# Hybrid block on one core: the attention's heads chained into one pipeline of key blocks, and the reciprocals of a query block spread over later steps

## The chip, the cores and the metric

One core of a Trainium2 chip runs the whole program. The metric is device time in microseconds; a run's time is that of one execution, and three runs of the kernel before are at hand. The engines are named as in the profile: PE (TensorE) does matmuls and PEld loads their stationary operand, DVE is VectorE, ACT is ScalarE, POOL is GpSimd, SP is SyncE, which here only issues DMAs. Each engine works off its own queue in order.

## The reference, cut to what matters

One decoder block on 1024 tokens of width 1024: a gated mix of an attention with forgetting and a state-space branch (S5), an output projection, then a mixture of 32 experts. The change touches only the attention, which has 8 heads of 64:

```python
qf = q * d ** -0.5                       # q, k normalised per head before
logits = einsum('bhqd,bhkd->bhqk', qb, kf) + cb[..., :, None] - cum[:, :, None, :]
logits = where(pos[None, :] <= pb[:, None], logits, -1e30)     # causal
p = softmax(logits, axis=-1)
o = einsum('bhqk,bhkd->bhqd', p, vf)
mixed = sigmoid(g_attn) * (y_attn @ w_proj_attn) + sigmoid(g_ssm) * (y_ssm @ w_proj_ssm)
```

## The kernel before, in words

Every fp32 product is made of parts: an operand is split into a high part, rounded to the fp32r type by ACT, and a low part, the rest, by DVE. Tiles whose names end in h (or H) and l (or L) are such pairs.

The attention works on four pairs of heads. For a pair, `proj` makes q, k and v of 128 tokens at a time (24 matmuls, L798 to L800, in a PSUM tile of `psA`); ACT and DVE take v out into the tile `V` (L809, L810). `prep` does one half of the tokens (512): it transposes k and q into two PSUM tiles of `psB` (L824, L827), ACT and DVE write them out as `KX`, `KY`, `QX`, `QY` (L836 to L842), and then it finds each query's largest logit, by matmuls into `psB` tiles (L855, with the causal mask L858) that DVE reduces (L860, tile `mx`); the maxima are transposed (L865), and POOL sends them by DMA into rows of `QX` (L871, L872).

`attend(pair, c)` takes the 512 queries of half c against 4c + 4 blocks of 128 keys, first for head a = 0 of the pair, then for a = 1. A unit of it is one key block: the logits in a `psB` tile (L904, L907, with the mask L906), two exponentials by ACT, `pH` (L910) and `pe` (L912; for the first block it goes to `sm`), the low part `pL` by DVE (L913), and the running sum of the exponentials, `sm`, by POOL (L915). The products with the values (L889 with `pH`, L890 with `pL`, summed in the `psA` tile `acc`) come three key blocks later, from a list `late`. At the end of a head the last three are emitted at once; then `yu` is written from `acc` (ACT L923, DVE L924), and `sm` is split into `sh` (ACT L926) and `sl` (DVE L928). After both heads, four matmuls (L933) with a selecting matrix sum `sh` and `sl` over the partitions into a tile of `psA`; DVE takes its reciprocals in four parts, each followed by a multiplication into `yu` (L936, L937); POOL stores `yu` to HBM (L944). `pL` and `sl` share four buffers, `yu` has one, `sm` two. `psA` and `psB` have four PSUM banks each.

`run_all` interleaves generators: each has a number of units and a stretch of the run [lo, hi], and the one whose next unit is due first goes on. One call runs `attend(cur, 0)` beside `proj` of the next pair and `prep(cur, 1)`, the next `attend(cur, 1)` beside `proj` and `prep` of the next pair. In the last pair the partner is `fill`: the products of the other branch's output (L703 to L705 with `wm` and `yhs`, DVE L728 writes `mixS`). After the last call come the products with `yha` (L703 to L705 again), of which the last key group needs the last pair's result (`y3`, DVE L942), and `emit_a` (DVE L991).

The code is not the order of the engines. A scheduler under it takes the instructions in program order as priority, models their times, gives out tile buffers and lets a later instruction pass one whose inputs or buffer are not there. So the place of an instruction in its engine's queue has to be read from the compiled program.

Of the kernel before, what the change touches and what calls it, by code (L numbers as in the profile page):

```python
# [10 lines left out]
F32 = mybir.dt.float32  # L11
# [31 lines left out]
def hybrid_block(ctx: ExitStack, tc: tile.TileContext, t, out):  # L43
# [728 lines left out]
    def new_pair(pr):  # L772
        p_ = Pair()
        p_.pr = pr
        p_.w = proj_weights(pr)
        p_.V = ap_.tile([P, NT, 2, 2, 64], F32R, name="V", bufs=2)
        p_.KX, p_.KY, p_.QX, p_.QY = [], [], {}, {}
        for a in range(2):
            kx = slot("KX", dt=F32R)
            ky = slot("KY", dt=F32R)  # L780
            nc.sync.dma_start(f32(kx[64:68, :]), negF_d[2 * pr + a])
            p_.KX.append(kx)
            p_.KY.append(ky)
        return p_

    def proj(p_, half):
# [4 lines left out]
        for r in range(4):  # L791
# [15 lines left out]
            vs = ps[:, 256:384].rearrange("p (a b) -> p a b", b=64)  # L807
            vh = p_.V[:, i, :, 0, :]
# [64 lines left out]

    def attend(p_, c, last=None):
# [3 lines left out]
        yu = ap_.tile([P, 512], F32, name="yu", bufs=1)  # L878
        sums = []
        for a in range(2):  # L880
            kx, qx, ky, qy = p_.KX[a], p_.QX[a, c], p_.KY[a], p_.QY[a, c]

            acc = psA.tile([P, 512], F32, tag="A", name="acc")
            sm = ap_.tile([P, 512], F32, name="sm", bufs=2)

            def values(kt, o0, n, pH, pL):
                v = p_.V[:, kt, a].rearrange("p a b -> p (a b)")
                o = acc[:, o0:o0 + n]
                nc.tensor.matmul(o, v, pH[:, :n], start=(kt == 0), stop=False)  # L889
                nc.tensor.matmul(o, v, pL[:, :n], start=False, stop=(kt == nkt - 1))  # L890

            late = []
            for kt in range(nkt):
# [17 lines left out]
                pe = ap_.tile([P, 512], F32, name="pe", bufs=3) if kt else sm  # L911
                nc.scalar.activation(pe[:, :n], ps[:, :n], AF.Exp)  # L912
                nc.vector.tensor_tensor(pL[:, :n], pe[:, :n], f32(pH[:, :n]), ALU.subtract)  # L913
                if kt:
                    nc.gpsimd.tensor_tensor(sm[:, o0:], sm[:, o0:], pe[:, :n], ALU.add)  # L915
# [6 lines left out]
            orow = slice(a * 64, a * 64 + 64)  # L922
            nc.scalar.copy(yu[orow, :], acc[0:64, :])  # L923
            nc.vector.tensor_tensor(yu[orow, :], yu[orow, :], acc[64:128, :], ALU.add)  # L924
            sh = ap_.tile([P, 512], F32R, name="sh", bufs=1)
            nc.scalar.copy(sh, sm)  # L926
            sl = ap_.tile([P, 512], F32R, tag="pL", name="sl", bufs=4)
            nc.vector.tensor_tensor(sl, sm, f32(sh), ALU.subtract)  # L928
            sums += [(a, sh), (a, sl)]
            yield  # L930
        ps = smtile() if last is not None else mmtile()
        for j, (a, v) in enumerate(sums):
            nc.tensor.matmul(ps, sel[:, a], v, start=(j == 0), stop=(j == 3))  # L933
        for q in range(4):
            qs = slice(q * P, q * P + P)
            nc.vector.reciprocal(ps[:, qs], ps[:, qs])  # L936
            nc.vector.tensor_tensor(yu[:, qs], ps[:, qs], yu[:, qs], ALU.mult)  # L937
        if last is not None:
            last.append((slot("yha", dt=F32R), slot("yla", dt=F32R)))
            yh, yl = last[-1]  # L940
            nc.scalar.copy(yh[:, 512:S], yu)
            nc.vector.tensor_tensor(yl[:, 512:S], yu, f32(yh[:, 512:S]), ALU.subtract)  # L942
            return
        nc.gpsimd.dma_start(yaT_d[p_.pr * P:(p_.pr + 1) * P, c * 512:c * 512 + 512], yu)  # L944
# [4 lines left out]
    for pr in range(4):  # L949
        if pr < 3:  # L950
            nxt = new_pair(pr + 1)
            run_all((attend(cur, 0), 10, 0.1, 1), (proj(nxt, 0), 12, 0, 1), (prep(cur, 1), 10, 0.25, 1))
            if pr < 2:
                run_all((attend(cur, 1), 18, 0.1, 1), (proj(nxt, 1), 12, 0, 1), (prep(nxt, 0), 10, 0.3, 1))
            else:
                fill = mixed_ssm()
                run_all((attend(cur, 1), 18, 0.1, 1), (proj(nxt, 1), 12, 0, 0.9), (prep(nxt, 0), 10, 0.3, 1),
                        (itertools.islice(fill, 5), 5, 0.9, 1.1))
# [593 lines left out]
```

## Time and profile before

| | |
|---|---|
| median of 3 runs | 1171.51 us (1167.63 to 1173.89) |
| the profiled execution | 1170.5 us, its span 1168.8 us, granted TensorE clock 0.981 |
| PE, PEld busy | 1106.3 us (95%), 848.5 us (73%) |
| DVE, ACT, POOL busy | 805.0 us (69%), 620.4 us (53%), 353.4 us (30%) |
| first and last logits of the attention (L904) | 356.2 and 635.7 us |
| experts | from about 840 us to the end |

The span runs from the first to the last instruction. A busy share is a mean over stages with different limits, so the stretch of the attention has to be asked for by itself. Matmuls overlap, so a matmul's duration is longer than the distance to the next one's start; idle time of PE stands in square brackets behind the row that ended it, with the releaser.

### The profile page before, as it was taken

The page shows a single profiled execution, that of the slowest core. Times are in us where ns is not written, and L with a number is a line of the kernel's source. Part 1 is how long each engine was busy: PE and PEld are TensorE (multiplying, and loading weights), DVE is VectorE, ACT ScalarE, POOL GpSimd, SP SyncE. Part 2 cuts the span into 40 slices and gives each one's busy share as a digit, 9 for nine tenths or more (in the row PEclk, how much of TensorE's full clock was granted, in tenths as well). Part 3 has the DMA queues.
Part 4 walks back from the last instruction along what each step waited for, and adds up shares of the span by engine and source line. Part 5 has one row for each costly group of instructions (what it writes and reads, how often), then busy time and mean ns, then how long its engine had stood idle before and what let it go on. Part 6 is the DMA issues. An engine that isn't in the chain of part 4 may idle for free. (4 is left out here: it accounts for less than half of the span.)

```text
span 1168.8 us, 15930 instructions
## 1 busy us (share of the span) xinstructions
PE 1106.3 (95%) x5323; PEld 848.5 (73%) x5324; DVE 805.0 (69%) x1594; ACT 620.4 (53%) x1195; POOL 353.4 (30%) x400
## 2 busy tenths in 40 slices
PE   6999999999999999999999989997799999999995
PEld 5787878887897888788667868786566666666562
DVE  6949878964147899898996795538666666666560
ACT  6433233333246666658878442113567777676562
POOL 4101011013144665747434351202222222222211
PEclk9999999999999999999999998999799999999998
DMA  8544553321704030002524548545899999999992
GB/s 250 78 110 120 129 82 83 82 73 54 153 17 55 12 65 11 16 10 82 208 82 136 183 152 299 182 164 200 281 330 339 321 314 308 316 312 320 320 335 50
DMA packets 100918, 193.78 MB, mean 166 GB/s; under 512 B 26176, under 2 KB 55168, under 8 KB 100832
## 3 DMA queue, kind: packets, MB, share of 16 engines
q1 hardware_dynamic: 82176, 150.16, 42.1%
q0 software_dynamic: 14048, 34.17, 10.8%
q10 hardware_dynamic: 4608, 8.39, 1.9%
q8 instruction: 43, 0.70, 0.2%
q14 instruction: 43, 0.35, 0.1%
HBM read 164.30 MB, written 35.52 MB: 171 GB/s over the span
## 5 line engine op out<-in xcount | busy, mean ns | idle before, releaser
L1126 DVE TENSOR_TENSOR wel<-raw_e,weh 128x512 fp32r<-128x512 f32 x248 | 152.3, 685 | 118.3 <-ACT weh L1125 114.5
L1125 ACT CAST weh<-raw_e 128x512 fp32r<-128x512 f32 x248 | 132.7, 623 | 1.6 <-DMA raw_e<-in_w_expert_up 1.5
L1404 PE MATMUL psA_t<-wd,hT 128*96 128x512 f32 x256 | 117.2, 600 | 2.8 <-DMA wd<-in_w_expert_down 2.0
L915 POOL TENSOR_TENSOR sm<-sm,pe 128x256 f32<-128x256 f32 (+2 forms) x80 | 96.2, 1202 | 68.6 <-ACT pe L912 60.4
L1379 PE MATMUL psA_t<-weh,xh 128*96 128x512 f32 x256 | 103.2, 403 | 0.2
L1380 PE MATMUL psA_t<-wel,xh 128*96 128x512 f32 x256 | 101.0, 395 | 0.0
L1381 PE MATMUL psA_t<-weh,xl 128*96 128x512 f32 x256 | 101.0, 394 | 0.0
L162 PE MATMUL psA_t<-hTl,wgh 128*128 128x512 f32 x256 | 100.6, 393 | 0.0
L161 PE MATMUL psA_t<-hTh,wgl 128*128 128x512 f32 x256 | 100.5, 393 | 0.0
L160 PE MATMUL psA_t<-hTh,wgh 128*128 128x512 f32 x256 | 100.4, 392 | 0.0
L798 PE MATMUL psA_t<-wqh,hTh 128*128 128x384 f32 x256 | 87.9, 343 | 0.0
L799 PE MATMUL psA_t<-wql,hTh 128*128 128x384 f32 x256 | 86.3, 337 | 0.0
L800 PE MATMUL psA_t<-wqh,hTl 128*128 128x384 f32 x256 | 86.2, 337 | 0.0
L1406 POOL DMA_INDIRECT out_rows<-R,ix x32 | 46.1, 1441 | 128.3 <-ACT hT L1395 117.1
L1405 ACT ACTIVATE R<-psA_t,wts 96x512 f32<-96x512 f32 x64 | 43.7, 682 | 77.0 <-PE psA_t L1404 74.9
L1404 PEld LDWEIGHTS psA_t<-wd,hT 128*96 128x96 f32 x256 | 40.4, 168 | 55.5 <-issue 50.4
L1355 POOL DMA_INDIRECT XG<-xn_d,ix x32 | 32.1, 1002 | 136.3 <-PE psB_t L1366 129.6
L910 ACT ACTIVATE pH<-psB_t 128x512 fp32r<-128x512 f32 (+1 forms) x96 | 49.3, 513 | 35.8 <-PE psB_t L907 35.6
L913 DVE TENSOR_TENSOR pL<-pe,pH 128x256 fp32r<-128x256 f32 (+2 forms) x80 | 62.6, 794 | 6.1 <-ACT pe L912 5.2
L164 ACT COPY ge<-psA_t 128x512 f32<-128x512 f32 x32 | 18.6, 582 | 70.1 <-PE psA_t L162 70.1
L161 PEld LDWEIGHTS psA_t<-hTh,wgl 128*128 128x128 f32 x256 | 48.1, 188 | 9.7
L160 PEld LDWEIGHTS psA_t<-hTh,wgh 128*128 128x128 f32 x256 | 48.1, 188 | 9.6
(429 smaller groups left out, 2845.5 us busy)
## 6 DMA issues: line engine op xcount, KB each, us to landing
raw_e<-in_w_expert_gate SPq DMA_DIRECT2D x64, 512.0 KB
raw_e<-in_w_expert_up SPq DMA_DIRECT2D x64, 512.0 KB
wd<-in_w_expert_down SPq DMA_DIRECT2D x64, 512.0 KB
gate_d<-ge ACTq DMA_DIRECT2D x32, 256.0 KB
gt<-gate_d SPq DMA_DIRECT2D x16, 512.0 KB
raw_g<-in_w_in SPq DMA_DIRECT2D x12, 512.0 KB
raw_q<-in_w_in SPq DMA_DIRECT2D x48, 128.0 KB
x<-in_x SPq DMA_DIRECT2D x8, 512.0 KB
```

What stands on the lines that cost most here:

```text
L160: nc.tensor.matmul(ps, wh, hTh[k][:, ns], start=(k == 0), stop=False)
L161: nc.tensor.matmul(ps, wl, hTh[k][:, ns], start=False, stop=False)
L162: nc.tensor.matmul(ps, wh, hTl[k][:, ns], start=False, stop=(k == KD - 1))
L798: nc.tensor.matmul(ps[:, :384], ah, wh, start=(k == 0), stop=False)
L799: nc.tensor.matmul(ps[:, :384], ah, wl, start=False, stop=False)
L915: nc.gpsimd.tensor_tensor(sm[:, o0:], sm[:, o0:], pe[:, :n], ALU.add)
L1125: nc.scalar.copy(wh[d_], src)
L1126: nc.vector.tensor_tensor(wl[d_], src, f32(wh[d_]), ALU.subtract)
L1379: nc.tensor.matmul(ps, xh[:, k, :], wh[:, k % 2, :], start=(k == 0), stop=False)
L1380: nc.tensor.matmul(ps, xh[:, k, :], wl[:, k % 2, :], start=False, stop=False)
L1381: last = nc.tensor.matmul(ps, xl[:, k, :], wh[:, k % 2, :], start=False, stop=(k == KD - 1))
L1404: pe = nc.tensor.matmul(po, hT[:, j, :], wd[j][:, ns], start=(j == 0), stop=(j == 1))
```

## The change

The list `late` is no longer a head's own: it goes across heads, calls of `attend` and pairs. So a head's last three products with the values are emitted in the first units of whatever head comes next. What followed them at the end of a head (`done`: `yu`, `sh`, `sl`) comes when the last of them has been emitted, and the sums over the partitions (`add_up`) are made for each head by itself: `sh` and `sl` of head 0 start a tile, those of head 1 finish it. That tile now comes from `psB` in all calls, not from `psA`. The four reciprocals with their multiplications are dealt out to the next four units (`later`), and the store of `yu` follows the last of them, which lies in the next call of `attend`. `yu` is taken from its one buffer when the first head is done; `V` when the first tokens of a pair are written. The last call drains the lists in units of its own. The numbers given to `run_all` change too: attention counts 8 and 16 units (24 in the last call), and the starts of the stretches move.

```diff
-        p_.V = ap_.tile([P, NT, 2, 2, 64], F32R, name="V", bufs=2)
+        p_.V = None
...
+            if p_.V is None:
+                assert all(v[0] >= p_.pr - 1 for v in late)
+                p_.V = ap_.tile([P, NT, 2, 2, 64], F32R, name="V", bufs=2)
...
+    late, later = [], []
+    def advance(depth):
+        while len(late) > depth:
+            late.pop(0)[1]()
+            if depth:
+                break
+        for v in list(later):
+            v[0] -= 1
+            if v[0] <= 0:
+                later.remove(v)
+                v[1]()
...
     def attend(p_, c, last=None):
-        yu = ap_.tile([P, 512], F32, name="yu", bufs=1)
-        sums = []
+        b = Block()
+        b.yu = None
+        def values(h, a, kt, o0, n, pH, pL):
+            if kt == 0:
+                h.acc = psA.tile([P, 512], F32, tag="A", name="acc")
...
+            if kt == nkt - 1:
+                done(h, a)
+        def done(h, a):
+            if b.yu is None:
+                b.yu = ap_.tile([P, 512], F32, name="yu", bufs=1)
+            orow = slice(a * 64, a * 64 + 64)
+            nc.scalar.copy(b.yu[orow, :], h.acc[0:64, :])
+            nc.vector.tensor_tensor(b.yu[orow, :], b.yu[orow, :], h.acc[64:128, :], ALU.add)
+            sh = ap_.tile([P, 512], F32R, name="sh", bufs=1)
+            nc.scalar.copy(sh, h.sm)
+            sl = ap_.tile([P, 512], F32R, tag="pL", name="sl", bufs=4)
+            nc.vector.tensor_tensor(sl, h.sm, f32(sh), ALU.subtract)
+            later.append([1, lambda: add_up(b, a, (sh, sl))])
+        def add_up(b, a, vs):
+            if a == 0:
+                b.ps = smtile()
+            for j, v in enumerate(vs):
+                nc.tensor.matmul(b.ps, sel[:, a], v, start=(a + j == 0), stop=(a + j == 2))
+            if a:
+                for q in range(4):
+                    later.append([1 + q, lambda q=q: scaled(b, q)])
+        def scaled(b, q):
+            qs = slice(q * P, q * P + P)
+            nc.vector.reciprocal(b.ps[:, qs], b.ps[:, qs])
+            nc.vector.tensor_tensor(b.yu[:, qs], b.ps[:, qs], b.yu[:, qs], ALU.mult)
+            if q == 3:
+                result(b)
...
-                late.append((kt, o0, n, pH, pL))
-                if len(late) > 3:
-                    values(*late.pop(0))
+                late.append((p_.pr, lambda h=h, a=a, v=(kt, o0, n, pH, pL): values(h, a, *v)))
+                advance(3)
                 yield
-            for v in late:
-                values(*v)
...
-        ps = smtile() if last is not None else mmtile()
-        for j, (a, v) in enumerate(sums):
-            nc.tensor.matmul(ps, sel[:, a], v, start=(j == 0), stop=(j == 3))
...
+        if last is not None:
+            while late or later:
+                advance(len(late) - 1 if len(late) > 1 else 0)
+                yield
...
-            run_all((attend(cur, 0), 10, 0.1, 1), (proj(nxt, 0), 12, 0, 1), (prep(cur, 1), 10, 0.25, 1))
+            run_all((attend(cur, 0), 8, 0, 1), (proj(nxt, 0), 12, 0.15, 1), (prep(cur, 1), 10, 0.25, 1))
-                run_all((attend(cur, 1), 18, 0.1, 1), (proj(nxt, 1), 12, 0, 1), (prep(nxt, 0), 10, 0.3, 1))
+                run_all((attend(cur, 1), 16, 0.05, 1), (proj(nxt, 1), 12, 0, 1), (prep(nxt, 0), 10, 0.3, 1))
...
-            run_all((attend(cur, 0), 10, 0, 1), (itertools.islice(fill, 16), 16, 0, 1),
+            run_all((attend(cur, 0), 8, 0, 1), (itertools.islice(fill, 16), 16, 0, 1),
-            run_all((attend(cur, 1, y3), 18, 0.1, 1), (fill, 32, 0, 1), (ready_a(), 5, 0.5, 0.95))
+            run_all((attend(cur, 1, y3), 16 + 8, 0, 1), (fill, 32, 0, 1), (ready_a(), 5, 0.5, 0.95))
```

What it does to the queues is shown at three places. In the rows below, a number behind a name tells buffers apart, and the changed program has line numbers of its own: the logits are L967 to L970, the products with the values L909 and L910, the sums L931, `yu` L918, `sh` L921, the reciprocals and multiplications L938 and L939, `pL` L976, the maxima L858 to L863.

PE, the end of the second pair's `attend(cur, 1)`, before:

```order
L855 MATMUL psB_t_4660<-KX_3885,QX_4401 128x512
L858 LDWEIGHTS identb_129
L858 MATMUL psB_t_4660<-mask_m_272,identb_129 128x128
L889 MATMUL acc_4481<-pH_4598,V_3032 128x384
L890 MATMUL acc_4481<-pL_4599,V_3032 128x384
L889 MATMUL acc_4481<-pH_4611,V_3032 128x256
L890 MATMUL acc_4481<-pL_4612,V_3032 128x256
L889 MATMUL acc_4481<-pH_4637,V_3032 128x256
L890 MATMUL acc_4481<-pL_4638,V_3032 128x256
L933 MATMUL psA_t_4676<-sh_4463,sel_2609 128x512
L933 MATMUL psA_t_4676<-sl_4465,sel_2609 128x512
L798 MATMUL psA_t_4740<-wqh_4698,hTh0_134 128x384
```

The same place in the changed program:

```order
L970 MATMUL psB_t_4714<-QX_4388,KX_3858 128x512
L799 MATMUL psA_t_4728<-wql_4676,hTh1_135 128x384
L800 MATMUL psA_t_4728<-wqh_4675,hTl1_143 128x384
L798 MATMUL psA_t_4728<-wqh_4683,hTh2_136 128x384
L799 MATMUL psA_t_4728<-wql_4684,hTh2_136 128x384
L800 MATMUL psA_t_4728<-wqh_4683,hTl2_144 128x384
L967 MATMUL psB_t_4738<-QY_4389,KY_3859 128x384
L969 LDWEIGHTS identb_129
L969 MATMUL psB_t_4738<-mask_s_267,identb_129 128x128
L970 MATMUL psB_t_4738<-QX_4388,KX_3858 128x384
L909 MATMUL acc_4554<-pH_4627,V_3111 128x256
L910 MATMUL acc_4554<-pL_4628,V_3111 128x256
```

Before, the head's last six products stand in a row, its last key block's right after the two ahead of it, and the sums (of head 0) come at once. Now the logits of the next call's first two key blocks (`psB_t_4714`, `psB_t_4738`) and parts of its `proj` lie ahead of the second last pair of products, and those of a third ahead of the last pair and of the sum of this head.

DVE, the reciprocals of that call, before:

```order
L869 SCALAR_TENSOR_TENSOR ml_4693<-psB_t_4690,mh_4692 4x128
L936 RECIPROCAL psA_t_4676<-psA_t_4676 128x128
L937 TENSOR_TENSOR yu_4271<-psA_t_4676,yu_4271 128x128
L936 RECIPROCAL psA_t_4676<-psA_t_4676 128x128
L937 TENSOR_TENSOR yu_4271<-psA_t_4676,yu_4271 128x128
L913 TENSOR_TENSOR pL_4767<-sm_4761,pH_4766 128x512
L936 RECIPROCAL psA_t_4676<-psA_t_4676 128x128
L805 TENSOR_REDUCE ss_4738<-psA_t_4740 128x4
L937 TENSOR_TENSOR yu_4271<-psA_t_4676,yu_4271 128x128
L811 TENSOR_SCALAR ss_4738<-ss_4738 128x4
L913 TENSOR_TENSOR pL_4790<-pe_4792,pH_4789 128x384
L936 RECIPROCAL psA_t_4676<-psA_t_4676 128x128
```

And in the changed program, the first two of the four:

```order
L938 RECIPROCAL psB_t_4523<-psB_t_4523 128x128
L813 TENSOR_TENSOR V_4800<-psA_t_4728,V_4800 128x2x64
L841 TENSOR_TENSOR QY_4816<-psB_t_4765,QX_4815 64x512
L842 SCALAR_TENSOR_TENSOR KY_3862<-psB_t_4760,gk2_279,KX_3861 64x512
L976 TENSOR_TENSOR pL_4839<-pe_4841,pH_4838 128x256
L939 TENSOR_TENSOR yu_4516<-psB_t_4523,yu_4516 128x128
L863 TENSOR_REDUCE mx_4850<-psB_t_4851 128x1
L863 TENSOR_REDUCE mx_4850<-psB_t_4854 128x1
L863 TENSOR_REDUCE mx_4850<-psB_t_4867 128x1
L863 TENSOR_REDUCE mx_4850<-psB_t_4870 128x1
L805 TENSOR_REDUCE ss_4726<-psA_t_4824 128x4
L938 RECIPROCAL psB_t_4523<-psB_t_4523 128x128
```

Before, the four stand within 13 rows with three other pieces of work between, on a tile of `psA`; now the second stands 11 rows behind the first, on a tile of `psB` that head 0's sum took while that call was still at head 1's logits, and reductions of the next call's maxima lie between.

ACT, the end of the second pair's first call, `attend(cur, 0)`, and the first exponentials of the next, before (in brackets the semaphores waited for; DMASW is a DMA that POOL issued):

```order
L910 ACTIVATE pH_4177<-psB_t_4173 128x256 [waits PE_49]
L912 ACTIVATE pe_4180<-psB_t_4173 128x256
L923 COPY yu_3910<-acc_4076 64x512 [waits PE_49]
L803 COPY qk_3888<-psA_t_4156 128x256 [waits PE_49]
L804 ACTIVATE psA_t_4156<-psA_t_4156 128x256
L926 CAST sh_4210<-sm_4077 128x512 [waits PE_49,Pool_49]
L809 CAST V_3881<-psA_t_4156 128x2x64 [waits DVE_49]
L868 ACTIVATE mh_4238<-psB_t_4236 4x128 [waits DMASW5_49,PE_49]
```

And in the changed program:

```order
L973 ACTIVATE pH_4195<-psB_t_4191 128x256 [waits PE_49]
L975 ACTIVATE pe_4198<-psB_t_4191 128x256
L803 COPY qk_3876<-psA_t_4165 128x256 [waits PE_49]
L804 ACTIVATE psA_t_4165<-psA_t_4165 128x256
L918 COPY yu_4145<-acc_3996 64x512 [waits DMASW1_49,DVE_49]
L921 CAST sh_4294<-sm_4039 128x512 [waits Pool_49]
L812 CAST V_3951<-psA_t_4165 128x2x64 [waits DVE_49,Activation_49]
L871 ACTIVATE mh_4229<-psB_t_4227 4x128 [waits DMASW5_49,PE_49]
```

The copy of `yu` stood behind the last products of head 1; now head 0's copy stands here, waits for the store of the `yu` before, and the maxima and the next call's exponentials are queued behind it.

More of the change, by code (lines that the diff above doesn't have):

```diff
@@ L879, in attend @@
-        sums = []
+        b = Block()
+        b.yu = None
+        b.sums = []
+        def values(h, a, kt, o0, n, pH, pL):
+            if kt == 0:
+                h.acc = psA.tile([P, 512], F32, tag="A", name="acc")
+            v = p_.V[:, kt, a].rearrange("p a b -> p (a b)")
+            o = h.acc[:, o0:o0 + n]
+            nc.tensor.matmul(o, v, pH[:, :n], start=(kt == 0), stop=False)
+            nc.tensor.matmul(o, v, pL[:, :n], start=False, stop=(kt == nkt - 1))
+            if kt == nkt - 1:
+                done(h, a)
@@ L880, in attend, with result @@
+        def result(b):
+            if last is not None:
+                last.append((slot("yha", dt=F32R), slot("yla", dt=F32R)))
+                yh, yl = last[-1]
+                nc.scalar.copy(yh[:, 512:S], b.yu)
+                nc.vector.tensor_tensor(yl[:, 512:S], b.yu, f32(yh[:, 512:S]), ALU.subtract)
+                return
+            nc.gpsimd.dma_start(yaT_d[p_.pr * P:(p_.pr + 1) * P, c * 512:c * 512 + 512], b.yu)
         for a in range(2):
             kx, qx, ky, qy = p_.KX[a], p_.QX[a, c], p_.KY[a], p_.QY[a, c]
-            acc = psA.tile([P, 512], F32, tag="A", name="acc")
@@ L884, in attend @@
[L884 to L892, printed above, removed]
+            h = Block()
+            h.sm = ap_.tile([P, 512], F32, name="sm", bufs=2)
             for kt in range(nkt):
@@ L914, in attend @@
                 if kt:
-                    nc.gpsimd.tensor_tensor(sm[:, o0:], sm[:, o0:], pe[:, :n], ALU.add)
-                late.append((kt, o0, n, pH, pL))
-                if len(late) > 3:
-                    values(*late.pop(0))
+                    nc.gpsimd.tensor_tensor(h.sm[:, o0:], h.sm[:, o0:], pe[:, :n], ALU.add)
+                late.append((p_.pr, lambda h=h, a=a, v=(kt, o0, n, pH, pL): values(h, a, *v)))
+                advance(3)
                 yield
-            for v in late:
-                values(*v)
[L922 to L930, printed above, removed]
-        ps = smtile() if last is not None else mmtile()
-        for j, (a, v) in enumerate(sums):
[L933 to L937, printed above, removed]
-        if last is not None:
[L939 to L944, printed above, removed]
+        if last is not None:
+            while late or later:
+                advance(len(late) - 1 if len(late) > 1 else 0)
+                yield
     cur = new_pair(0)
@@ L951, in hybrid_block @@
             nxt = new_pair(pr + 1)
-            run_all((attend(cur, 0), 10, 0.1, 1), (proj(nxt, 0), 12, 0, 1), (prep(cur, 1), 10, 0.25, 1))
+            run_all((attend(cur, 0), 8, 0, 1), (proj(nxt, 0), 12, 0.15, 1), (prep(cur, 1), 10, 0.25, 1))
             if pr < 2:
-                run_all((attend(cur, 1), 18, 0.1, 1), (proj(nxt, 1), 12, 0, 1), (prep(nxt, 0), 10, 0.3, 1))
+                run_all((attend(cur, 1), 16, 0.05, 1), (proj(nxt, 1), 12, 0, 1), (prep(nxt, 0), 10, 0.3, 1))
             else:
                 fill = mixed_ssm()
-                run_all((attend(cur, 1), 18, 0.1, 1), (proj(nxt, 1), 12, 0, 0.9), (prep(nxt, 0), 10, 0.3, 1),
+                run_all((attend(cur, 1), 16, 0.05, 1), (proj(nxt, 1), 12, 0, 0.9), (prep(nxt, 0), 10, 0.3, 1),
                         (itertools.islice(fill, 5), 5, 0.9, 1.1))
```

4 lines of the change are left out of this document (3 added, 1 removed).

## The prediction

> **What bounds the kernel now.** I read the page first, then the attention's stretch by windows, then PE's waits there, and last the queues around one wait. Page, busy time of each engine:
>
> ```profile
> span 1168.8 us, 15930 instructions
> PE 1106.3 (95%) x5323; PEld 848.5 (73%) x5324; DVE 805.0 (69%) x1594; ACT 620.4 (53%) x1195; POOL 353.4 (30%) x400
> ```
>
> PE is without work for 1168.8 - 1106.3 = 62.5 us of the span. Stretches (busy us of each engine with instructions, granted clock, share of the DMA engines, GB/s): the attention, the products behind it, the stretch up to the output projection, most of the experts.
>
> ```profile
> core 0: us, PE busy (x) PEld busy (x) DVE busy (x) ACT busy (x) POOL busy (x), PEclk, DMA share, GB/s
> 356.00:640.00 284.00, 270.88 (x1441) 223.22 (x1440) 247.62 (x434) 201.99 (x412) 159.44 (x166) 0.99 0.23 65
> 640.00:656.00 16.00, 16.00 (x72) 13.21 (x72) 11.22 (x23) 7.29 (x11) 1.93 (x8) 1.00 0.36 98
> 656.00:700.00 44.00, 39.50 (x165) 31.43 (x163) 40.67 (x57) 21.14 (x43) 25.72 (x16) 0.96 0.56 191
> 840.00:1080.00 240.00, 240.00 (x1006) 150.57 (x1005) 148.97 (x264) 167.98 (x336) 58.12 (x48) 1.00 0.99 320
> ```
>
> In the attention PE idles 284.0 - 270.9 = 13.1 us: that is all the room in the stretch, 1.1% of the time. DVE is busy 87% there, so it is no bound by its sum, but little late work is needed for PE to wait for it. Whose waits PE's idle time is (us in all, times, longest), in the same stretch:
>
> ```profile
> PE acc L890 <- DVE pL L913: 4.4, 9, 0.9
> PE psA_t L933 <- DVE mixS L728: 1.4, 1, 1.4
> PE psB_t L855 <- ACT KY L842: 1.3, 3, 0.5
> PE psB_t L865 <- DVE mx L863: 1.3, 2, 0.7
> PE psB_t L855 <- DVE mx L860: 1.1, 1, 1.1
> PE acc L889 <- ACT pH L910: 0.7, 2, 0.4
> PE psB_t L865 <- DVE mx L860: 0.6, 1, 0.6
> PE psA_t L703 <- ACT wm L686: 0.6, 1, 0.6
> PE psA_t L704 <- DVE wm L687: 0.5, 1, 0.5
> ```
>
> The first and sixth rows, 5.1 us, are the products with the values. One of these waits, at the end of the second pair's second call, on PE and on DVE (start, duration, idle time in brackets):
>
> ```profile
> 490.33 0.28 PE L889 MATMUL acc<-pH,V 128*128 128x256 f32 x1
> 491.25 0.39 PE L890 MATMUL acc<-pL,V 128*128 128x256 f32 x1 [0.64 <-DVE pL L913]
> ...
> 485.70 3.21 DVE L913 TENSOR_TENSOR pL<-pe,pH 128x384 fp32r<-128x384 f32 x2
> 488.83 1.49 DVE L768 TENSOR_TENSOR wql<-raw_q,wqh 128x768 fp32r<-128x768 f32 x1
> 490.25 0.55 DVE L860 TENSOR_REDUCE mx<-psB_t 128x1 f32<-128x384 f32 x1
> 490.71 0.48 DVE L913 TENSOR_TENSOR pL<-pe,pH 128x256 fp32r<-128x256 f32 x1
> ```
>
> DVE had no gap from 485.70 on; the last `pL` came at 491.19, and PE, which emits the last three key blocks at once, stood before it. The same happens at other heads' ends.
>
> **The change, part by part.** No matmul, exponential, reciprocal or DMA is added or removed; only places change.
>
> (1) *The last three products of a head go behind the next head's logits.* The order shows two scores and some of `proj` ahead of the second last. The waits for `pL` and `pH` go: 5.1 us. Bounds: 0 (DVE is as late three units on) and 5.1; I take 5.1, since in the rows above DVE was under 1 us late (longest 0.9) and the products now stand some 20 matmuls later.
>
> (2) *The sum leaves `psA`.* The wait of L933 for `mixS` is one for a bank of `psA` in the fourth pair. It goes: 1.4 us (bounds 0 and 1.4, since `proj` or `acc` could meet that bank instead).
>
> (3) *The sum holds a bank of `psB`.* Calls begin, by their first logits, at
>
> ```profile
> 427.80 0.40 PE L904 MATMUL psB_t<-QY,KY 128*128 128x512 f32 x1
> 456.69 0.48 PE L904 MATMUL psB_t<-QY,KY 128*128 128x512 f32 x1
> 496.16 0.40 PE L904 MATMUL psB_t<-QY,KY 128*128 128x512 f32 x1
> ```
>
> so `attend(., 0)` lasts 28.9 us and `attend(., 1)` 39.5. Head 0's sum starts in unit 11 of 16, and the last reciprocal is in unit 7 of the next call's 8: held for 5/16 x 39.5 + 7/8 x 28.9 = 37.6 us. The other call's: 1/8 x 28.9 + 7/16 x 39.5 = 20.9. Of a pair's 68.4 us the logits and maxima have three banks instead of four for 58.5. No row shows three banks. The nearest is the fifth wait above: PE once waited 1.1 us for a reduction of maxima to free a bank. Lower bound 0 (the scheduler puts matmuls of `proj` between); upper bound: 88 tiles of maxima in the stretch,
>
> ```profile
> L860 DVE TENSOR_REDUCE mx<-psB_t 128x1 f32<-128x512 f32 (+2 forms) x88 | 47.3, 556 | 3.6 <-PE psB_t L855 1.6 <-PE psB_t L858 1.3
> L936 DVE RECIPROCAL psA_t<-psA_t 128x128 f32<-128x128 f32 x28 | 26.8, 959 | 2.0 <-PE psA_t L933 1.8
> ```
>
> each fourth of which waits for one reduction: 22 x 0.556 = 12.2 us. I take two more waits like the nearest row's, 2.2 us.
>
> [...]
>
> (4) *The reciprocals are dealt out.* Four of them with their multiplications take DVE 4 x (0.959 + 0.28) = 5.0 us (the multiplication's row is quoted under the tail). The order shows that they already stood among `pL` and other work, so little is gained: 0. Bounds: a gain of 1.9, the two rows in which the maxima's transposition L865 waits for DVE; a loss of 1.9, as much again, since reductions of maxima now stand behind reciprocals.
>
> (5) *The store of `yu` moves into the next call; the copy of the next `yu` waits for it.* In three calls (`attend(., 0)` of pairs 2 to 4) it is close, with the exponentials queued on ACT behind the copy.
>
> ```profile
> L944 POOL DMA_DIRECT2D yaT_d<-yu x7: 574/586/623, 395.9 to 608.7; - x7
> ...
> DMA to landing us min/median/max: 2.3/2.7/4.2
> ```
>
> Store issue 0.6 and landing 2.7 us, after the last multiplication. ACT reaches the copy after the last two exponentials and two pieces of 0.4 us, which need head 1's last logits, so the two come at about the same time, and PE has a dozen matmuls of `proj` and maxima meanwhile. Bounds 0 and 3 x (0.6 + 4.2) = 14.4; I take 0.3 us, since PE feels only what outlasts them. POOL, which issues the store in order, makes `sm` wait behind it for 0.6 us; the units are 2.5 us or more apart, so that is covered.
>
> (6) *`run_all`'s numbers, `V` taken late, four L933 as two and two:* no instruction more; 0, bounds -1.1 and +1.1, the two rows on `wm`, which wait for weights whose loads change places on SP.
>
> (7) *The tail.* Before, the last reciprocals lie under 72 matmuls of the window 640 to 656, in which PE has no gap:
>
> ```profile
> 648.98 0.29 DVE L937 TENSOR_TENSOR yu<-psB_t,yu 128x128 f32<-128x128 f32 x1
> 649.96 0.69 DVE L942 TENSOR_TENSOR yla<-yu,yha 128x512 fp32r<-128x512 f32 x1 [0.69 <-ACT yha L941]
> ```
>
> The result is there at 650.65, and the products that need it come at about 656. So an earlier end of the attention gains nothing by itself (0), but what PE saved before 640 goes through: 640 to 656 is PE's, DVE starts the emitting when PE delivers, and the experts, with PE busy 240 of 240 us and DMA at 0.99, move as a whole since their loads follow the same buffers.
>
> Of the 6.5 us some comes back because DVE, at 87%, is asked for the same 247.6 us in less time. I set 0 for it, and leave it to the rivals.
>
> Sum: -5.1 - 1.4 + 2.2 + 0 + 0.3 + 0 + 0 = -4.0 us. The profiled execution took 1170.5 us (its span plus 1.7), 1.0 below the median 1171.51; against the median the forecast is 1167.5, against the execution 1166.5. The three runs lie 6.3 us apart, so less than 0.5%, 5.9 us, can't be told from no change.
>
> **The rivals.**
>
> *DVE is late wherever PE stands.* The waits for `pL` go, but PE meets DVE at the maxima and at `V` instead. For it: DVE's 87%, and 3.21 us for two `pL` of width 384 in the rows above. Against: 36 us without DVE work in the stretch. Then 5.1 comes back nearly whole: about 1171.
>
> *Three banks of `psB` are too few (slower).* The place: `prep`, whose two transposed tiles hold two banks until DVE and ACT have written `KX` to `QY`; with the sum in a third, logits have one bank, and the maxima after it two. The price: 0.556 us for each tile of maxima that waits; it outweighs part (1) and (2) from 6.5 / 0.556 = 12 waits on, and is measurable from (6.5 + 5.9) / 0.556 = 22 on. At 28 waits (a third of the 88) it is 15.6 - 6.5 = +9.1: 1180.6. For it: the hold of 58.5 of 68.4 us. Against: only two PE waits for a bank with four.
>
> *More than the products' waits go.* The scores of a new head no longer stand behind the old head's end, so the maxima's chain and `KY` (rows three, four and seven: 3.2 us) lose theirs too, and nothing comes back: -6.5 - 3.2 = -9.7: 1161.8. For it: `proj` is at hand at each boundary. Against: those rows wait for `prep`, which isn't touched.
>
> **How the numbers follow.** Forecast 0.45 (of that 0.12 past the bound of 5.9 us, 0.33 within); DVE late 0.18 (within); too few banks 0.18 (slower); more goes 0.19 (faster). Two hundredths of "too few banks" are small enough to stay within; so faster 0.31, same 0.53, slower 0.16. The likeliest case's own range is 1163 to 1171 (from -8 to -0.5). The range for 8 in 10 takes in "more goes" (1161.8, a little below it) and half of "too few banks": 1160 to 1178.
>
> **What would show it.** Right: PE's wait of L910 (now the products with `pL`) for `pL` under 1 us in the stretch; no wait of the sum L931 for `mixS`; PE's idle time in the attention about 9 us; the attention's last logits some 4 us or more earlier; DVE's busy time there unchanged at about 248 us. The second rival shows as PE waits of logits or maxima (L967, L858) for DVE `mx` or ACT `pe` of over 10 us; the first as waits for DVE of other lines, with the sum of PE's idle time at 13; ACT's copy L918 waiting for the DMA into `yaT_d`, by more than 2 us at a time, would refute part (5). The forecast is wrong if the stretch's PE busy time itself grows, which nothing here prices.

## The result and the profile after

| | before | after |
|---|---|---|
| median, same comparison | 1171.07 us | 1184.0 us (1182.15 to 1188.93) |
| ratio, 95% interval | | 1.0137 [1.0114, 1.0159] |
| the profiled execution, span | 1170.5, 1168.8 us | 1188.93, 1187.2 us |
| first product with `yha` (the attention is done) | 640.8 us | 657.1 us |
| from there to the end of the span | 528.0 us | 530.1 us |

The change makes the kernel slower, by 12.9 us between the medians and by 13 to 19 us by the interval of the ratio; the forecast was 1167.5, in a range of 1160 to 1178. The profiled execution is the slowest of the four after, so its trace shows 18.4 us of difference in the span, 16.3 of it in the stretch of the attention, which is where to look. Windows of the kernel before and of the changed kernel, from 356 us to the first product with `yha` (busy us of PE, PEld, DVE, ACT and POOL with instructions, granted clock, DMA share, GB/s):

```profile
356.00:640.80 284.80, 271.68 (x1445) 223.90 (x1444) 248.28 (x434) 202.24 (x413) 159.44 (x166) 0.99 0.23 66
```

```profile
356.00:657.10 301.10, 281.16 (x1453) 229.02 (x1452) 255.82 (x439) 204.16 (x416) 165.04 (x167) 0.97 0.21 60
```

PE idles 301.1 - 281.2 = 19.9 us instead of 13.1. It is also busy 9.5 us longer, for eight matmuls more in the trace, mostly since the clock is lower. PE's waits in the stretch (us, times, longest):

```profile
PE psB_t L931 <- DVE sl L923: 8.3, 9, 2.7
PE psB_t L858 <- ACT pe L975: 3.1, 2, 2.4
PE psB_t L868 <- DVE mx L863: 2.5, 3, 1.1
PE psB_t L967 <- ACT pe L975: 2.0, 3, 1.5
PE psB_t L858 <- ACT QY L844: 1.8, 3, 0.8
```

The waits of the products with the values for `pL` (4.4 before) and of the sum for `mixS` (1.4) are gone. In their place PE waits for `sl`, in the sum that is made one unit after `sl` was asked for, and for exponentials to free banks. The longest wait, in the second call of the last pair, on PE, DVE and POOL (start, duration, idle in brackets):

```profile
613.64 0.39 PE L704 MATMUL psA_t<-yhs,wm 128*128 128x512 f32 x1
613.86 0.39 PE L705 MATMUL psA_t<-yls,wm 128*128 128x512 f32 x1
...
614.68 0.39 PE L909 MATMUL acc<-pH,V 128*128 128x512 f32 x1
617.78 0.79 PE L931 MATMUL psB_t<-sl,sel 128*128 128x512 f32 x1 [2.71 <-DVE sl L923]
618.37 0.63 PE L910 MATMUL acc<-pL,V 128*128 128x512 f32 x1
618.80 0.63 PE L703 MATMUL psA_t<-yhs,wm 128*128 128x512 f32 x1
619.23 0.63 PE L704 MATMUL psA_t<-yhs,wm 128*128 128x512 f32 x1
...
612.22 0.69 DVE L728 TENSOR_TENSOR mixS<-psA_t,gt 128x512 f32<-128x512 f32 x1
612.83 3.23 DVE L976 TENSOR_TENSOR pL<-pe,pH 128x512 fp32r<-128x512 f32 x2
615.98 1.75 DVE L923 TENSOR_TENSOR sl<-sm,sh 128x512 fp32r<-128x512 f32 x1
617.65 1.76 DVE L976 TENSOR_TENSOR pL<-pe,pH 128x512 fp32r<-128x512 f32 x1
...
612.52 6.34 POOL L978 TENSOR_TENSOR sm<-sm,pe 128x512 f32<-128x512 f32 x4 [1.04 <-ACT pe L975]
```

Four units follow each other closely here. POOL's four running sums run back to back for 6.3 us, and beside them each of DVE's subtractions takes 1.6 to 1.76 us, where the one before (`mixS`, one input from PSUM) takes 0.69. The sum needs `sl` and stands ahead of product L910 and of `fill` (L703) in PE's queue, so all of them wait. Behind the wait, products of 512 columns start 0.43 us apart (618.80, 619.23); before it, 0.22 (613.64, 613.86). The windows around it show the granted clock at half:

```profile
617.00:624.00 7.00, 6.22 (x16) 4.74 (x17) 6.78 (x10) 1.50 (x3) 2.29 (x3) 0.51 0.08 19
624.00:627.00 3.00, 3.00 (x16) 2.41 (x15) 2.24 (x3) 2.97 (x3) 0.82 (x1) 1.00 0.32 130
```

In windows of 1 us the clock is either 1 or 0.5 but for the edges. Before, one piece of 3.4 us is at half; after, pieces of 3.4, 6.8 and 6.8 us, so 8.6 us are lost instead of 1.7. The difference of the stretch is then: idle time 19.9 - 13.1 = 6.8, halved clock 6.9, the rest (301.1 - 19.9 - 8.6 = 272.6 against 270.0) 2.6, together 16.3. (About 1 us of the long pieces lies in PE's idle time and is counted in both.) The other long piece at half clock lies where the last pair begins. PE, after:

```profile
574.29 0.39 PE L967 MATMUL psB_t<-QY,KY 128*128 128x256 f32 x1 [1.47 <-ACT pe L975]
574.52 0.28 PE L969 MATMUL psB_t<-mask_s,identb 128*128 128x256 bf16 x1
574.55 0.36 PE L970 MATMUL psB_t<-QX,KX 68*128 68x256 f32 x1
577.35 0.79 PE L858 MATMUL psB_t<-KX,QX 66*128 66x512 f32 x1 [2.43 <-ACT pe L975]
...
578.80 0.80 PE L703 MATMUL psA_t<-yhs,wm 128*128 128x512 f32 x1 [0.23 <-ACT wm L686]
```

There is no `proj` any more and `fill` has not begun (its first product is that of 578.80): the next matmul in the queue needs a bank that ACT has still to read.

### The profile page after: what moved, and what is told of

Same layout as the page of the kernel before. It is cut to its first block, busy times and chain, and to the rows that moved or that the text cites. A ratio compares the mean times of both kernels' runs of the same rounds, so it can differ in the third digit from the quotient of the medians.

```text
span 1187.2 us, 15939 instructions
## 1 busy us (share of the span) xinstructions
PE 1112.9 (94%) x5323; PEld 850.1 (72%) x5324; DVE 809.0 (68%) x1594; ACT 618.8 (52%) x1193; POOL 356.8 (30%) x400
## 5 line engine op out<-in xcount | busy, mean ns | idle before, releaser
L976 DVE TENSOR_TENSOR pL<-pe,pH 128x256 fp32r<-128x256 f32 (+2 forms) x80 | 67.2, 843 | 10.3 <-ACT pe L975 9.7
L863 DVE TENSOR_REDUCE mx<-psB_t 128x1 f32<-128x512 f32 (+2 forms) x96 | 50.5, 548 | 7.2 <-PE psB_t L861 3.8
```

## The experiments

The theories at the start: (T1) the sum stands too close behind `sl`, and DVE, which took 1.6 to 1.76 us for each subtraction beside POOL's sums in the rows above, is late for it; (T2) the sums hold a bank of `psB`; (T3) the new numbers of `run_all` crowd the units; (T4) reciprocals dealt out do harm. Later: (T5) the chain itself crowds; (T6) the order before is a good one among its neighbours, and any edit that moves the queues costs some per cent.

All results in one table. Idle is PE's from 356 us to the first product with `yha`; halved is what the half clock took there, added up from windows of 5 us; rest is the stretch less both. The last column is idle plus halved in 20 us around the last pair's start (from 14 us ahead of the first product with `yhs` to 6 behind). Where PE idles at half clock, up to 1.8 us for a kernel, the time is in both columns. These columns are of one profiled execution each.

| kernel | median us | ratio to before [95%] | first `yha` | idle | halved | rest | last pair's start |
|---|---|---|---|---|---|---|---|
| before | 1168.9 to 1171.1 | | 640.8 | 13.1 | 1.7 | 270.0 | 4.6 |
| n2: before, `prep` from 0.30 | 1168.6 | 0.9984 [0.9963, 1.0005] | 638.6 | 12.0 | 0.0 | 270.6 | 3.5 |
| n3: before, start 0.08 | 1169.64 | 0.9993 [0.9974, 1.0013] | 643.4 | 14.8 | 1.7 | 270.9 | 4.5 |
| e1_delay1: sum one unit later | 1175.55 | 1.0047 [1.0028, 1.0067] | 648.0 | 17.1 | 3.4 | 271.4 | 8.2 |
| n1: before, 11 units | 1178.54 | 1.0066 [1.0042, 1.009] | 654.7 | 22.0 | 8.5 | 268.2 | 14.4 |
| x1: delay1, `prep` from 0.30 | 1179.52 | 1.0072 [1.0046, 1.0098] | 652.4 | 18.4 | 8.5 | 269.4 | 9.3 |
| n4: after, 17 units | 1179.96 | 1.0084 [1.0055, 1.0113] | 655.5 | 22.5 | 6.8 | 270.2 | 9.8 |
| e14b: delay1, last pair spread | 1180.7 | 1.0091 [1.0059, 1.0123] | 652.4 | 17.3 | 10.2 | 268.9 | 10.4 |
| e11: both sums together | 1182.3 | 1.0107 [1.0091, 1.0124] | 654.5 | 20.6 | 5.1 | 272.8 | 9.2 |
| after | 1184.0 | 1.0137 [1.0114, 1.0159] | 657.1 | 19.9 | 8.6 | 272.6 | 8.6 |
| e12: chain undone | 1184.19 | 1.0129 [1.0102, 1.0156] | 653.8 | 22.6 | 5.2 | 270.0 | 10.4 |
| e1_delay2: sum two units later | 1184.22 | 1.0133 [1.0112, 1.0154] | 652.8 | 22.4 | 5.1 | 269.3 | 7.9 |
| e6: before, sum in `psB` | 1184.47 | 1.0142 [1.0108, 1.0176] | 653.2 | 20.4 | 10.2 | 266.5 | 15.3 |
| e2: sum in `psA` | 1184.85 | 1.0113 [1.0064, 1.0162] | 653.4 | 22.9 | 1.7 | 272.8 | 6.4 |
| x2: x1, sum in `psA` | 1186.11 | 1.0116 [1.0089, 1.0143] | 654.4 | 22.2 | 5.2 | 271.1 | 9.3 |
| e4: old numbers | 1188.34 | 1.0132 [1.0083, 1.0181] | 658.3 | 22.4 | 10.2 | 269.6 | 11.6 |
| e3: reciprocals at once | 1191.53 | 1.0168 [1.0127, 1.0209] | 658.3 | 25.1 | 5.2 | 272.0 | 7.7 |
| e5: before, new numbers | 1198.2 | 1.0238 [1.021, 1.0266] | 666.9 | 27.1 | 10.2 | 273.6 | 8.6 |

**One part at a time, from the changed kernel.** T1, the sum one unit later and two:

```diff
-            later.append([1, lambda: add_up(b, a, (sh, sl))])
+            later.append([2, lambda: add_up(b, a, (sh, sl))])   # e1_delay1; 3 in e1_delay2
```

> The changed kernel, but a head's sum over the partitions (L931) is emitted one unit later. Theory 'late low part' (PE's queue has the sum with sl at a place that DVE, slowed by POOL's adds, reaches too late: 8.3 us of PE waits, and a lower granted clock after the longest of them): those waits fall below 3 us, the clock holds near 615 us, and the time falls by 8 to 11 us, to about 1174. Theory 'banks' (the sum's long hold of a psB bank): no change, 1184, or slower, since sl now holds one of the four pL buffers a unit longer. Theory 'shares' (the new numbers of run_all): no change, 1184.

> The changed kernel with a head's sum two units later. Theory 'late low part': PE's waits of L931 for sl, 6.0 us with one unit, fall below 2 us, and the time to about 1171, as much as before the change. Rival 'pL ring' (sl now keeps one of the four buffers of pL for two units more, so the products with the values come nearer to their pL): L910 waits for pL by 3 us or more, and the time stays at 1175 or rises.

One unit more took 8.4 us off the median, but not as T1 had it: PE still waits 6.0 us for `sl`, not under 3, and most of what the trace saves is halved clock (3.4 instead of 8.6 us). Two units took nothing off, though the wait in question nearly went; nor does L910 wait for `pL` (0.3 us), so the buffers of `pL` aren't it either. PE's waits with two units:

```profile
PE psB_t L967 <- ACT pe L975: 5.7, 4, 1.7
PE psB_t L868 <- DVE mx L863: 5.2, 3, 2.9
PE psB_t L858 <- ACT pe L975: 2.6, 2, 2.4
...
PE psB_t L931 <- DVE sl L923: 1.2, 1, 1.2
```

`sl` fell from 8.3 to 1.2, and logits (for exponentials) and transposed maxima (for reductions) wait instead: idle 22.4. So taking away the wait that the list names first doesn't take away the idle time: DVE and ACT are late, and whatever PE has next stands before it.

T2, the sum in `psA` (e2), and both heads' sums together when the second is done, which holds the bank for a shorter time (e11):

```diff
-                b.ps = smtile()
+                b.ps = mmtile()     # e2
...
-            later.append([1, lambda: add_up(b, a, (sh, sl))])
+            b.sums.append((sh, sl))     # e11
+            if a:
+                later.append([1, lambda: [add_up(b, j, v) for j, v in enumerate(b.sums)]])
```

> The changed kernel with the sum's tile in psA again (held as long). Theory 'banks': PE's waits of logits and maxima for ACT pe (5.1 us) go, and with them the low clock near 577 us (about 3.5 us): 1175. Theory 'late low part': the waits of L931 for sl stay at about 8 us, and the time within 3 us of 1184. Theory 'shares': 1184.

> The changed kernel with the sums of both heads emitted together when head 1 is done, as before the change (still in psB, reciprocals still dealt out, products with the values still chained). Theory 'late low part': only head 0's half of the waits of L931 goes, head 1's sum still follows its sl at once: about 4 us of waits left and 1179. Theory 'banks': the hold falls from 58 to some 25 us of a pair's 68; if banks matter after all, 1175 or less.

Neither gives the time back: 1184.85 and 1182.3. In e2's trace the waits for `pe` fall from 5.1 to 1.7 us and the halved clock to 1.7, as its expectation had it, but idle time grows to 22.9. T2 falls for the changed kernel as what its time hangs on.

T4 and T3, the reciprocals at once (e3) and the numbers of `run_all` as before (e4):

```diff
-                    later.append([1 + q, lambda q=q: scaled(b, q)])
+                    scaled(b, q)        # e3
...
-            run_all((attend(cur, 0), 8, 0, 1), (proj(nxt, 0), 12, 0.15, 1), ...   # and the others
+            run_all((attend(cur, 0), 10, 0.1, 1), (proj(nxt, 0), 12, 0, 1), ...   # e4
```

> The changed kernel with the four reciprocals emitted together, right after the sum, so that the psB bank is held some 27 us of a pair's 68 instead of 58. Theory 'banks': about half of its 9 us comes back, 1179. Theory 'late low part': L931 waits as long, 1184 within 3. If dealing out the reciprocals was itself a gain, it is slower than 1184.

> The changed kernel with run_all's old numbers (attention 10 and 18 units from 0.1 on, proj from 0). Theory 'shares': most of the 13 us comes back, 1173. Theories 'late low part' and 'banks': within 4 us of 1184, with waits of L931 for sl and of logits for ACT pe as before.

Neither is faster, so T3 and T4 fall. The medians are 7.5 and 4.3 us higher, but both intervals of the ratio overlap that of the change, so that the three can't be told apart.

**POOL's sums.** Both kernels without the line that adds `pe` to `sm` on POOL. The attention's values are then others, and with them the experts' load, so that only the stretch of the attention is compared:

```diff
-                if kt:
-                    nc.gpsimd.tensor_tensor(h.sm[:, o0:], h.sm[:, o0:], pe[:, :n], ALU.add)
...
-            nc.scalar.copy(sh, h.sm)
+            nc.scalar.activation(sh, h.sm, AF.Copy, bias=1.0)
...
-            nc.vector.tensor_tensor(sl, h.sm, f32(sh), ALU.subtract)
+            nc.vector.tensor_tensor(sl, h.sm, f32(sh), ALU.max)
```

> The changed kernel without POOL's running sum over the key blocks (left out; sh and sl are made of the first block's exponentials plus one, so that no division by zero comes up). Theory 'late low part through POOL': pL (L976) and sl (L923) take about 0.69 us at width 512 instead of up to 1.75, PE's waits of L931 for sl fall from 8.3 to under 2 us, and the time to 1170 or less; its distance to the same cut in the kernel before is under 5 us. Rival 'place alone' (the sum stands too near behind sl whatever DVE's speed): waits of 5 us or more stay, and the distance is 10 us or more.

> The kernel before with the same cut: no running sum by POOL. Both theories: PE's wait for pL at heads' ends shrinks, 1166 to 1170. It is the measure for the cut in the changed kernel.

Windows up to the first product with `yha`, the changed kernel's first:

```profile
356.00:634.60 278.60, 271.45 (x1448) 225.59 (x1447) 226.63 (x440) 205.72 (x418) 65.02 (x86) 0.99 0.22 65
```

```profile
356.00:630.90 274.90, 268.61 (x1458) 225.51 (x1457) 222.97 (x439) 202.87 (x415) 64.23 (x87) 1.00 0.24 68
```

The distance falls from 16.3 to 3.7 us, idle is 7.2 and 6.3 us, and no wait for `sl` is left. `pL` of width 512, in the changed kernel, without POOL's sums, and in the kernel before (busy, mean ns of one):

```profile
L976 DVE TENSOR_TENSOR pL<-pe,pH 128x512 fp32r<-128x512 f32 x32 | 35.4, 1110 | 6.8 <-ACT pe L975 6.8
```

```profile
L976 DVE TENSOR_TENSOR pL<-pe,pH 128x512 fp32r<-128x512 f32 x32 | 22.9, 717 | 7.8 <-ACT pe L975 7.7
```

```profile
L913 DVE TENSOR_TENSOR pL<-pe,pH 128x512 fp32r<-128x512 f32 x32 | 27.5, 874 | 2.7 <-ACT pe L912 2.4
```

So most of the distance goes with POOL's sums. That it is their work beside DVE's alone isn't shown, since leaving them out moves the queues too, and one part of the loss stays without them, at the last pair's start. Windows of 20 us there, without POOL's sums, the changed kernel's first:

```profile
550.50:570.50 20.00, 15.99 (x74) 12.07 (x74) 18.68 (x31) 18.76 (x37) 3.46 (x4) 0.83 0.66 237
```

```profile
547.70:567.70 20.00, 18.94 (x105) 15.24 (x105) 18.77 (x35) 18.00 (x37) 6.78 (x8) 1.00 0.79 284
```

Idle time and halved clock are 7.4 us there (4.0 and 3.4) against 1.1; with POOL's sums they are 8.6 against 4.6. PE waits for ACT there as in the rows at 574.29 and 577.35 above:

```profile
560.23 0.39 PE L967 MATMUL psB_t<-QY,KY 128*128 128x256 f32 x1 [1.58 <-ACT pe L975]
562.55 0.80 PE L858 MATMUL psB_t<-KX,QX 66*128 66x512 f32 x1 [1.69 <-ACT pe L975]
```

Nor do these two runs tell which part of the change brings POOL's sums and DVE's subtractions together more often.

**One part alone, from the kernel before, and the chain undone.** In e12 `late` is emptied at each head's end; in e6 only the sums' bank is changed, in e5 only the numbers; e14b is e1_delay1 with 10 and 20 units in the last pair.

```diff
+            while late:                 # e12, after the loop over a head's key blocks
+                late.pop(0)[1]()
...
-        ps = smtile() if last is not None else mmtile()
+        ps = smtile()                   # e6, in the kernel before
...
-            run_all((attend(cur, 0), 10, 0.1, 1), (proj(nxt, 0), 12, 0, 1), ...     # and the others
+            run_all((attend(cur, 0), 8, 0, 1), (proj(nxt, 0), 12, 0.15, 1), ...     # e5, in the kernel before
...
-            run_all((attend(cur, 1, y3), 16 + 8, 0, 1), ...
+            run_all((attend(cur, 1, y3), 20, 0, 1), ...                             # e14b; attend(cur, 0) 10 for 8
```

> The changed kernel, but the list of late products is emptied at the end of every head, as in the kernel before: no product with the values goes into the next head's units. The sums still come head by head, one unit later, in a psB bank, with the reciprocals dealt out. Two theories. (A) The sum standing one unit behind the sl it needs, with DVE slowed by POOL's adds, is what costs: then it stays at 1180 to 1187 us, with at least 5 us of waits of L931 for sl. (B) The chain itself costs, because it packs the products of one head and the first units of the next into the same few us of DVE and ACT: then most of the 13 us goes, 1171 to 1175 us, and the distance to the first product with yha, 16.3 us longer than before in the changed kernel, falls under 5.

> The kernel before with one edit: the sums of every call go into a bank of psB instead of psA (except the last, which always did). Held only from both heads' end to the fourth reciprocal, so for less time than in the change. Theory of the banks: three banks for logits and maxima cost, at least +5 us, 1176 or more, with waits of L855, L904 for DVE mx or ACT pe growing by 4 us. Theory of the late low part: the bank is no part of it, 1169 to 1173 us, and the wait of 1.4 us of L933 for mixS is gone.

> The kernel before with only the numbers of the interleaving changed (attention counts 8 and 16 units, 24 in the last call, the stretches begin as in the change). In the changed kernel the new numbers were worth 4 us against the old. If they are good by themselves: 1166 to 1169 us. If they only fit the chain: 1171 to 1175. In the last call 24 units for 16 pack the attention into the first two thirds, so that DVE should be met late there: waits of the products for pL in 600 to 640 us, over 2 us more than before, if packing units is what makes DVE late.

> The variant with the sum one unit later (1175.55 us) with one more edit: in the last pair attention counts 10 and 20 units instead of 8 and 24, so that its units stand farther apart between the products of fill. If it is the packing of units that lets POOL's adds run back to back and DVE's subtractions with them, the last pair, which took 6.6 us more than before, gets 3 to 5 back: 1170 to 1173 us. If the last pair's loss comes from elsewhere (its first calls' maxima and casts without fill at hand), 1174 to 1177.

Undoing the chain (e12) saves nothing, so T5 falls; the time is the one that T1 gives, but its waits for `sl` aren't there, and PE waits for `sh` instead (4.8 us). With its bank alone in `psB` the kernel before is 15 us slower, with the numbers alone 29 (1166 to 1175 us was expected), where in the changed kernel taking the bank back saved nothing and the old numbers couldn't be told from the new. The parts don't add up. e14b, meant to give 3 to 5 us back, is at 1180.7 outside both of its ranges. e5's waits for `pL` in its last call are 0.5 us, not over 2: T3's reason wasn't its cause. And e6's waits aren't for a bank that is held:

```profile
PE psB_t L855 <- ACT QY L841: 4.7, 4, 2.0
PE psB_t L933 <- ACT sh L926: 3.8, 1, 3.8
PE acc L890 <- DVE pL L913: 3.2, 5, 1.1
PE psA_t L703 <- ACT wm L686: 2.1, 1, 2.1
```

**Neutral shifts.** T6 was put to the test with edits that are no part of the change:

```diff
-            run_all((attend(cur, 0), 10, 0.1, 1), ..., (prep(cur, 1), 10, 0.25, 1))
+            run_all((attend(cur, 0), 11, 0.1, 1), ..., (prep(cur, 1), 10, 0.25, 1))    # n1; n2: 10 units, prep from 0.3
...
-                run_all((attend(cur, 1), 18, 0.1, 1), ...
+                run_all((attend(cur, 1), 18, 0.08, 1), ...                             # n3
...
-                run_all((attend(cur, 1), 16, 0.05, 1), ...
+                run_all((attend(cur, 1), 17, 0.05, 1), ...                             # n4, in the changed kernel
```

> The kernel before with one number changed: attend(cur, 0) beside proj counts 11 units instead of 10. It moves units by a fraction of one and is none of the change's parts. If the change's parts cost by what they do (a bank held, a sum close behind its low part), a neutral shift costs little: 1168 to 1175. If the order before is a fitted one, and the scheduler's next best order is some per cent worse whatever the edit, this too is slower, 1178 or more.

> The kernel before with one number changed: prep(cur, 1) begins at 0.30 of its call instead of 0.25. Again none of the change's parts. Parts cost by themselves: 1168 to 1175. Fitted order: 1178 or more.

> The kernel before with one number changed: attend(cur, 1) beside proj begins at 0.08 instead of 0.10. The smallest shift of the three. Parts cost by themselves: 1169 to 1174. Fitted order: 1174 or more.

> The changed kernel with one number changed: attend(cur, 1) beside proj counts 17 units instead of 16. If the loss of the change is a property of its structure, it stays within 1181 to 1187. If the level is that of an order that was not fitted, such a shift moves it by as much as the edits of single parts did, 5 us or more in either direction.

Two of three shifts of the kernel before make no difference that can be told, the third costs 0.66%, and its waits are those of e6:

```profile
PE psB_t L855 <- ACT QY L841: 6.6, 4, 2.5
PE psA_t L933 <- ACT sh L926: 3.8, 1, 3.8
PE acc L890 <- DVE pL L913: 2.8, 4, 1.1
PE psA_t L703 <- ACT wm L686: 2.6, 1, 2.6
```

So e6's 15 us can't be put down to the bank: an edit that leaves the bank alone brings the same four waits, nearly the same halved clock (8.5 against 10.2 us), 6.8 us of it in both at the last pair's start. Windows of 20 us around the last pair's start, of the kernel before, the changed kernel and n1:

```profile
553.60:573.60 20.00, 17.22 (x83) 13.21 (x84) 19.20 (x32) 14.23 (x30) 14.29 (x14) 0.91 0.68 238
```

```profile
564.80:584.80 20.00, 14.82 (x64) 10.40 (x63) 19.04 (x29) 17.87 (x34) 9.36 (x10) 0.83 0.67 237
```

```profile
568.90:588.90 20.00, 12.35 (x42) 9.60 (x41) 14.73 (x23) 14.43 (x25) 8.48 (x10) 0.66 0.63 229
```

T6 is half right: an order can be moved without loss (n2, n3), and one small shift cost 9 us. For the changed kernel a shift gave 4 us back (n4, between its two forecasts), so differences of that size between variants of it are no evidence on its parts.

**Two variants of e1_delay1.** Both start `prep(cur, 1)` at 0.30; x2 also has the sums in `psA`.

> The changed kernel with the sum one unit later (1175.55 us) and prep(cur, 1) from 0.30 of its call on, which left the kernel before at 1168.60. If the late start of prep is good for the chain too (its transposes meet fewer units of the old head): 1168 to 1173. If shifts of one number act by the order they happen to give, with no gain of their own: anywhere in 1172 to 1184. In either case the stretch from 356 us to the first product with yha should be 268 to 273 us plus PE's idle time plus what the halved clock takes.

> As the one beside it, and the sums in a bank of psA in all calls. If the bank in psB costs (15 us in the kernel before), this is faster than the one beside it by 3 us or more; if it only did so by the order it gave, within 5 us of it on either side. The same sum of 268 to 273 us, idle time and halved clock is expected.

x1's median is 4 us above that of e1_delay1, x2's another 6.6, and the intervals of neighbours overlap: a loss by the bank of `psB` can't be seen. The rest of the stretch is 269.4 and 271.1 us, as expected. No version beat the kernel before; n2 and n3 can't be told from it.

## Why the prediction was wrong

What it said of most of the named places came true; the sum did not.

- Parts (1) and (2), the waits taken away: right. L910 waits for `pL` not at all in the list after, and no L931 waits for `mixS`. But 5.1 and 1.4 us weren't gained, because PE waited for DVE and ACT elsewhere in its queue, for `sl` alone 8.3 us.
- Part (3), the bank, 2.2 us: the waits that it named (logits and maxima for `pe` or `mx`) grew from 1.1 to 5.8 us (3.1 + 2.0 + 0.5 + 0.2), twice the growth that it took and under its bound of 12.2; giving the bank back brought no time (e2, x2). Most of PE's idle time here isn't that: 8.3 of the 19.9 us are waits for `sl`, and e6, which holds the bank only from both heads' end on, lost 15 us with waits for `sh`, `QY` and `pL`.
- Part (4), 0 within 1.9: open. With the reciprocals at once (e3) the median is 7.5 us higher, but the intervals overlap, and e3 moves the order too.
- Part (5), 0.3: right. ACT's copy of `yu` waits for the store 1.1 us in all:

```profile
ACT yu L918 <- DMA yaT_d<-yu: 1.1, 2, 0.5
```

- Part (6), 0 within 1.1: wrong as a part by itself. The numbers alone cost the kernel before 29 us (e5); with the rest of the change, old and new can't be told apart (e4).
- Part (7): right within 2.1 us. From the first product with `yha` to the end it is 528.0 and 530.1 us.

The step that failed is the sentence behind the parts: "Of the 6.5 us some comes back because DVE, at 87%, is asked for the same 247.6 us in less time. I set 0 for it". DVE wasn't busy for the same time: up to the first product with `yha` it took 255.8 us instead of 248.3, since more subtractions ran beside POOL's sums (the `pL` of 512 columns took 35.4 us instead of 27.5), and the wait for `sl`, with PE one unit behind it, had no price at all; it measured 8.3 us. The rival "DVE is late wherever PE stands" was right in kind, but it was capped at what was gained, 5.1 us; PE's idle time grew by 6.8 beyond what it had been. And the sum had no term for the clock: the waits grew in length, to 2.4 and 2.7 us, and each long one came with 6.8 us at half speed, another 6.9 us in all. Nor did the range allow for what moving the queues does by itself, which part (6) put at 1.1 us at most: the shift of one number in n1, none of the change's parts, cost the kernel before 9. The prediction named a growth of the stretch's PE busy time as what would make it wrong; it grew by 9.5 us, mostly through the halved clock.

Shown: the loss lies in the attention's stretch, as idle time of PE and the halved clock after it; in all 18 kernels of the table the rest is 266.5 to 273.6 us while the two together go from 12 to 37; most of it goes when POOL's sums are left out, an edit that moves the queues too; and some of it, with or without POOL's sums, comes at the last pair's start (3.5 to 4.6 us in the three good orders, 6.4 to 15.3 in all others; the change's own 13.7 us of idle time and halved clock have 4.0 there). Not settled: how much of the 13 us is the chain's own, and how much the order that these numbers happened to give. The spread of neutral shifts is 0 to 9 us before and one of 4 us after. What speaks for a cost of its own, without showing it, is that none of the 11 variants of the changed kernel with POOL's sums came under 1.0047.

## What to carry to other kernels

Where a planner sets the order of full queues, the price of an edit isn't the sum over its parts: shift a number that means nothing, once or twice, to learn what reordering alone does to the time, and widen the range by it, towards slower where the order at hand does better than its neighbours. A wait that is named isn't work that can be saved: ask which engine is late and what PE has next in its queue. And price bunched idle time of PE with the half clock behind it: here 1.7 us for a piece of 3.4 us, and two waits of under 1 us, close together, stood ahead of it before (0.92 and 0.83 us) as one of 2.71 us did after.

## What the hardware showed

The half clock came in pieces of 3.4 us or a multiple, of 3.4 to 13.7 us in the attention's stretch of the table's kernels. In the trace after it came behind idle time that was no whole piece of 3.4 us long: PE worked until 615.07 us, waited 2.71, and was at half speed from about 617.1 to 624. Ahead of the other long piece it worked 0.63 of 3 us:

```profile
574.00:577.00 3.00, 0.63 (x3) 0.39 (x3) 2.94 (x4) 2.90 (x7) 1.42 (x1) 0.86 1.03 388
577.00:583.00 6.00, 5.42 (x12) 3.85 (x13) 5.81 (x10) 5.92 (x10) 0.73 (x1) 0.50 0.56 210
583.00:586.00 3.00, 3.00 (x15) 2.47 (x14) 2.97 (x4) 2.94 (x5) 0.00 (x0) 1.00 0.00 0
```

In each run with more than one piece in the stretch, the pieces begin on one grid of 3.41 us (after, at 559.10, 576.17 and 617.13 us: 5 and 12 steps apart), so the steps of this grid can be compared. Three of them, of the kernel before, the changed kernel and e3:

```profile
557.99:561.40 3.41, 1.66 (x9) 0.87 (x8) 3.41 (x9) 1.37 (x4) 2.58 (x3) 1.00 0.84 284
```

```profile
613.71:617.12 3.41, 1.36 (x7) 0.62 (x5) 3.41 (x3) 2.76 (x6) 3.25 (x3) 1.00 0.00 0
```

```profile
613.77:617.18 3.41, 1.72 (x8) 0.97 (x7) 3.41 (x3) 3.04 (x7) 3.25 (x3) 1.00 0.00 0
```

Half clock followed the first, which has only two short waits (0.92 and 0.83 us), and the second, but not the third, where L931 waited for `sl` as long as in the second (2.70 us), but with 1.69 us of the wait inside the step instead of 2.05. In the attention's stretch of all 20 traces, PE was busy for 0.69 to 2.08 us of the step ahead of a piece at half clock, once for 2.44; of the steps at full clock with less than 1.7 us, all were followed by one, and of those with 1.7 to 2.1 us 17 of 43. So the length of a wait didn't settle it: the counts go with how much PE worked within one step, and so with where on the grid the wait fell.

DVE's subtractions of 128x512 with both inputs in SBUF, taken singly from the trace after: 0.71 us in the mean for the 28 that met no sum of POOL, 1.17 for the 36 that met one, 1.82 at most; before, 40 met none (0.69 us) and 24 one (0.94). The sums' 128x512 took 1.465 us in the mean before and 1.573 after; of the 32 after, the 29 that met one of DVE's subtractions took 1.60 and the 3 that met none 1.29, so both sides took longer together.
